# First v weights prepared one unit earlier, and the sample rows' first loads of groups 1 and 2 placed two ticks later

## The chip, the cores and the metric

One core of one Trainium2 chip runs the whole program. The metric is the device time of one execution in microseconds (us); lower is better.

## The reference

One layer of a hybrid decoder is computed for a prompt (1 x 1024 tokens) and for 8 sample sequences of 4 tokens with caches, both with the same weights, width 1024. In short:

```python
h = rmsnorm(x)
q, k, v, z, xbc, dt = split(h @ w_in)
# attention: 12 heads x 64 in 3 dilation groups of 4; per-head RMS norm of q, k; ALiBi;
# (window, dilation) = (128,1), (512,4), (2048,16); the groups are combined by softmax denominators
o_g, lse_g = dilated_attn(q_g, k_g, v_g)       # prompt: blocks of 128; sample: cached keys and values
att = concat(o_g * softmax_g(lse_g))
# SSD: conv(4) + SiLU on xbc, chunked scan (8 chunks, 2 groups), D skip, SiLU(z) gate, norm
y = rmsnorm((ssd(silu(conv(xbc)), dt) + D * xs) * silu(z))
x = x + concat(att, y) @ w_out
x = x + ConvFFN(rmsnorm(x))                    # up, conv(3), SiLU gate, down
```

Outputs are both y, the new key and value rows, the SSM states and the convolution tails.

## The kernel before

Every large product is made of three float32r products: a matrix is split into a high part (`hi`, a cast on ScalarE) and a low part (`lo = raw - hi` on VectorE), and hi·hi, hi·lo and lo·hi are accumulated.

**The projection to q, k, v** is six *slices*: qk and v of group 0, qk and v of group 1, qk and v of group 2. In a slice 9 *units* follow each other (`ORDER`: first the 32 sample rows, then 8 tiles of 128 prompt rows); a unit is 24 matmuls (16 for the sample rows) into one `p_mm` bank (`qkv_unit`). In slice 0 the activations are transposed and split too (`x_load`, `x_tile`). While a slice runs, the weights of the next one are loaded in four quarters (`wq_load`, on SyncE's queue SP) and split in pieces (`wq_split`): 4 pieces for v weights (cast L439 to `wvh`, subtraction L440 to `wvl`), 8 for qk weights (`wqkh`, `wqkl`). In slice 0 the loads of the first v weights come with n = 3 to 6 and the four pieces with n = 5 to 8. VectorE also runs the norms: L615 (sum of squares of a unit), then GpSimd L402 and L403 (rsqrt), then L620 and L621 on VectorE.

**Side work.** Attention, the sample rows and the scan are generators in `Side`. Each `tick` advances every active generator by one `yield`, in the order in which their names were added; what follows a `yield True` is run by the next `pre`, just ahead of the next tick. A qk slice has two ticks in a unit (one in the unit of the sample rows), a v slice one, and each chunk of the later stages three, one behind each third of 24 matmuls. So the order of all instructions is fixed when the program is written; a queue works in that order and never skips.

**Attention of a group** begins with `group_end(g)`: for groups 0 and 1 behind unit n = 1 of the next group's qk slice, for group 2 behind the last v slice, ahead of the xBC chunks. It loads the first two q, k, v tiles of groups 1 and 2 (`qt`, from the scratch `qscr`). `att_gen` then takes one tile: load `qt`, transposes (L670, L671), scores (L686, L689), bias and maximum (L696, with L699 on VectorE), exponentials (L702, ScalarE), transposes of the probabilities (L711), their copies `PT` (L717, L719), the product with v (L727). In group 2 a tile begins with every tick from the third on: tile 2 loads its `qt` in the fifth tick and is transposed in the sixth.

**The sample rows** of a group are `samp_gen(g)`; one runs at a time (width 1). It loads q (`sq_q`, 512 KB: 128 x 1024 f32), a bias (`bl`) and tiles of cached keys (`kt`, 512 KB each, three buffers). One tile of keys takes a GpSimd multiplication (L844), one `yield`, and a VectorE reduction (L846); group 1 has 9 such tiles and group 2 has 3. Then comes a softmax (L814 to L819, with ScalarE's L818), and the same number of value tiles with L851 and L855. Its result goes to `oscr` (L861). `samp_comb` joins the three groups; when it and the attention are through, `comb_gen` runs, and its end (`done.add("att")`) lets the SSD scan begin (`ssd_go`).

`samp_gen(1)` has its first tick right behind `group_end(1)`, `samp_gen(2)` in the third tick behind `group_end(2)`; in the same tick "samp" is advanced ahead of "att", and "kvout" (copies of the new keys and values, L1153) behind it.

**After the scan's first half.** The xBC projection is 12 chunks, then 8 z chunks follow; ahead of z chunk 2 stands a loop that runs ticks with no chunk's matmuls until the SSD of the first head group and its gate are through (`z_chunk`). The scan starts one sequence chunk every two ticks, and one every tick once the last xBC chunk is through (`ssd_go(1)`).

Below, a1, a2, ... are the ticks behind `group_end(1)` (a14 is the last of the qk slice, a15 to a23 those of the v slice), and x1, x2, ... the ticks of the xBC and z chunks and of that loop, from `group_end(2)` on.

Of the kernel before, what the change touches and what calls it, by code (L numbers as in the profile page):

```python
# [302 lines left out]
def body(tc, A):  # L303
# [101 lines left out]
    def r_store(r, scr):  # L405
        ps = p_st()
        T.transpose(ps[:9, :128], r, ident)
        rT = R("rT")
        AC.copy(rT, ps[:9, :128])
        SP.dma_start(scr[0:S].rearrange("(i p) -> i p", p=128), rT[:8])  # L410
        SP.dma_start(scr[S:NT].rearrange("(o p) -> o p", o=1), rT[8:9, :NS])


    def wq_bufs(kind, g):

        n = 512 if kind == "qk" else QN if g == 0 else 256
        return [[None, lo, n, raw] for raw, lo in (R("wqkl" if kind == "qk" else "wvl") for hf in range(2))]

    def wq_load(w, kind, g, q):

        raw = w[q // 2][3][:, q % 2 * 2:q % 2 * 2 + 2]
        src = A["w_in"][0, q * 256:(q + 1) * 256, :].rearrange("(k p) c -> p k c", p=128)
        if kind == "qk":
            for e in range(2):
                c0 = e * 768 + g * 256
                SP.dma_start(raw[:, :, e * 256:(e + 1) * 256], src[:, :, c0:c0 + 256])
        else:
            c0 = 1536 + g * 256
            SP.dma_start(raw[:, :, :256], src[:, :, c0:c0 + 256])
            if g == 0:  # L430
                SP.dma_start(raw[:, :, 256:QN], src[:, :, WIN - 16:WIN])

    def wq_split(w, hf, kks, kind, engine=None):
        _, lo, n, raw = w[hf]
        if w[hf][0] is None:
            w[hf][0] = R("wqkh" if kind == "qk" else "wvh")
        hi = w[hf][0]
        c = slice(kks[0], kks[-1] + 1)
        AC.copy(hi[:, c, :n], raw[:, c, :n])  # L439
        (engine or V).tensor_tensor(lo[:, c, :n], raw[:, c, :n], f32(hi[:, c, :n]), op=ALU.subtract)  # L440

    def pieces(kind):

        if kind == "qk":
            return [(hf, (k,)) for hf in range(2) for k in range(4)]
        return [(hf, (k, k + 1)) for hf in range(2) for k in (0, 2)]
# [3 lines left out]
    def x_load(i):  # L450
        rows = 128 if i < 8 else NS
        xt = R("xt")
        src = A["x_prompt"][0, i * 128:(i + 1) * 128, :] if i < 8 else A["x_sample"].rearrange("b t d -> (b t) d")
        SP.dma_start(xt[:rows], src)
        xts[i] = xt
# [3 lines left out]
    def x_save():  # L459
        while saves:  # L460
            SP.dma_start(*saves.pop(0))

    def x_tile(i):
        rows = 128 if i < 8 else NS
        x_save()
        xt = xts.pop(i)
        c0 = i * 128
        jk = R("jk")
        AC.activation(jk[:rows], xt[:rows], AF.Square, accum_out=ss[:rows, i:i + 1])
        rsqrt_mean(rtok[:, i:i + 1], ss[:, i:i + 1], D, 1)  # L470
        for kk in range(2):
            ps = p_st()
            for j in range(4):
                T.transpose(ps[:, j * 128:j * 128 + rows], xt[:rows, (kk * 4 + j) * 128:(kk * 4 + j + 1) * 128],
                            ident[:rows, :rows])
            pv = ps.rearrange("p (j c) -> p j c", j=4)[:, :, :rows]
            ks = slice(kk * 4, kk * 4 + 4)
            sx = R("sx")[:, :, :rows]
            V.tensor_tensor(sx, pv, g_in[:, ks, None].to_broadcast([128, 4, rows]), op=ALU.mult)
            xr = R("xr")[:, :, :rows]  # L480
            AC.copy(xr, pv)
            saves.append((xscr[:, ks, c0:c0 + rows], xr))
            h = X[0][:, ks, c0:c0 + rows]
            AC.copy(h, sx)
            (V if kk else G).tensor_tensor(X[1][:, ks, c0:c0 + rows], sx, f32(h), op=ALU.subtract)
        if i == 8:
            for p in range(2):
                V.tensor_copy(xsp[:, :, p, :], X[p][:, :, S:NT])
# [141 lines left out]
    def flush(keep=0):  # L630
        while len(stores) > keep:
            d, s = stores.pop(0)
            SP.dma_start(d, s)
# [127 lines left out]
    def per_b(src):  # L761
        return raw_ap(src, 0, [[1024, NB], [0, 16], [1, 1024]])

    def samp_gen(g):
        U = U_S[g]
        q = R("sq_q")
        SP.dma_start(q, per_b(qs[g][0]))
        bl = R("bl")
# [6 lines left out]
        def load(w, c):  # L775
            kt = R("kt")
            if g == 0 and c == 3:
                SP.dma_start(kt[:, :256], raw_ap(qs[0][1 + w], 0, [[256, NS], [0, 4], [1, 256]]))
            elif g == 0:
                n = U0[c + 1] - U0[c]  # L780
                SP.dma_start(kt[:, :n * 256], raw_ap(A["cache_kv0"], w * 256 + U0[c] * 512,
                                                     [[8 * 512, 128], [512, n], [1, 256]]))
            elif c == U - 1:
                SP.dma_start(kt, per_b(qs[g][1 + w]))
            else:
                SP.dma_start(kt, raw_ap(A[f"cache_kv{g}"], w * 256 + c * DIL[g] * 512,
                                        [[32 * 512, 128], [512, 4], [1, 256]]))
            return kt

        order = [(w, c) for w in range(2) for c in range(4 if g == 0 else U)]  # L790
        queue = list(order)
        tiles = {}

        def ahead(n):
            while queue and len(tiles) < n:
                w, c = queue[0]
                if w and c == (3 if g == 0 else U - 1) and ("row", g, 2) not in done:
                    return
                tiles[queue.pop(0)] = load(w, c)

        ahead(1)
        yield
        if g:
            ahead(2)
            yield
            yield
        for w, c in order:
            while (w, c) not in tiles:
# [4 lines left out]
            if w == 1 and c == 0:  # L813
                V.tensor_tensor(sc[:, :U * 16], sc[:, :U * 16], bl[:, :U * 16], op=ALU.add)  # L814
                sv = sc[:, :U * 16].rearrange("p (u e) -> p e u", e=16)
                V.tensor_reduce(m[:, 0:16], sv, op=ALU.max, axis=AX.X, negate=True)
                V.tensor_tensor(sv, sv, m[:, 0:16, None].to_broadcast([128, 16, U]), op=ALU.add)
                AC.activation(sc[:, :U * 16], sc[:, :U * 16], AF.Exp)  # L818
                V.tensor_reduce(m[:, 16:32], sv, op=ALU.add, axis=AX.X)  # L819
                yield  # L820
            if g == 0:
                n = U0[c + 1] - U0[c]
# [340 lines left out]
    for sl, (kind, g) in enumerate(slices):  # L1163
        nxt = slices[sl + 1] if sl < 5 else None
        todo = pieces(nxt[0]) if nxt else []
        for n, i in enumerate(ORDER):
            q = n - (3 if sl == 0 else 0)
            if nxt and q == 0:
                W[nxt] = wq_bufs(*nxt)
            if nxt and 0 <= q < 4:  # L1170
                wq_load(W[nxt], *nxt, q)
            if sl == 0:
                if n + 4 < 9:
                    x_load(ORDER[n + 4])
                if n + 2 < 9:
                    x_tile(ORDER[n + 2])
                if n == 8:
                    x_save()
                    r_store(rtok, rscr)
            qkv_unit(kind, g, i)  # L1180
            flush(2)
            if nxt and n >= (5 if nxt[0] == "v" else 2):
                for _ in range(1 if nxt[0] == "v" or n < 8 else 2):
                    if todo:
                        wq_split(W[nxt], *todo.pop(0), nxt[0])
            if sl == 5:
                if n == 0:
                    stc = R("stc")
                    side.add("states", [states_in("st_in", stc, "state_conv", 24, 4, 12)], 1)
                if n in (1, 3):  # L1190
                    w_load(n // 2)
                if n in (5, 6):
                    w_split(0, n - 5, False)
                if n in (6, 7):
                    w_split(0, n - 6, True)
            side.tick()
            if n == 1 and g and kind == "qk":
                group_end(g - 1)
            if (kind, g) == ("qk", 1) and n == 3:
                side.add("dt", [dt_gen()])  # L1200
            if sl == 1 and n == 0:
                samp_rows(0, 1)
            if sl and n == 4:
                samp_rows(g, 1 if kind == "qk" else 2)
        assert not todo
        if sl == 0:
            side.add("cols", [cols_load()], 1)
        del W[kind, g]
# [678 lines left out]
def build(tc, nc, A):  # L1887
    body(tc, A)
# [24 lines left out]
```

## Time and profile before

| | us |
|---|---|
| three runs | 1652.19, 1644.55, 1650.20 |
| their median | 1650.2 |
| the profiled execution, its own time | 1650.86 |
| its span, first to last instruction | 1648.8 |
| what lies around the span | 2.06 |
| TensorE busy | 1605.4 (97%) |
| VectorE, ScalarE, GpSimd busy | 1010.4, 612.9, 365.0 |
| mean granted TensorE clock | 0.987 of full |

TensorE is the engine that is nearly always busy, so a change counts where TensorE stands still or has its clock lowered. "L711 <- ACT P L702" is to be read as: the instruction of line 711 waited for what ScalarE's line 702 wrote into P. In rows of single instructions the first number is the start, the second the duration; what stands in brackets is how long the engine had been idle before it and which instruction ended that.

### The profile page before, as it was taken

To read this page: it belongs to the slowest core of one execution; us is meant where nothing else is said; L and a number is where in the kernel's file an instruction comes from. 1 tells how busy PE (TensorE), PEld (TensorE's weight loads), DVE (VectorE), ACT (ScalarE), POOL (GpSimd) and SP (SyncE) were. 2 spreads that over 40 slices of the span, in tenths; PEclk is the share of its full clock that TensorE was granted. 3 is DMA by queue.
4 is the path that set the end of the run, shared out by engine and by line. 5 is a ranking of instruction groups with operands and counts; after the bars stand their busy time and mean duration, and the time that the engine had idled before them with its cause. 6 is when DMAs were issued, how large, how long until landed. Compare 5 with 4: busy or idle time off the path is not lost.

```text
span 1648.8 us, 26426 instructions
## 1 busy us (share of the span) xinstructions
PE 1605.4 (97%) x10543; PEld 1520.0 (92%) x10543; DVE 1010.4 (61%) x1714; ACT 612.9 (37%) x1140; POOL 365.0 (22%) x400
## 2 busy tenths in 40 slices
PE   7999998989999899899999999999999999999998
PEld 5787886988998789799999999999999999999998
DVE  5657748656678877753554565564655647555565
ACT  6535524446377874332332322122222221312221
POOL 4554336411025774310111000000000000000000
PEclk9999998999999999899999999999999999999999
DMA  7562366584322317652113111102121020211102
GB/s 231 155 177 75 116 190 198 185 208 125 94 83 85 103 52 208 183 173 67 43 54 103 40 53 39 53 27 65 31 61 53 26 65 14 78 40 39 53 1 106
DMA packets 173897, 154.66 MB, mean 94 GB/s; under 512 B 19554, under 2 KB 152058, under 8 KB 173775
## 3 DMA queue, kind: packets, MB, share of 16 engines
q1 hardware_dynamic: 173775, 152.98, 31.2%
q8 instruction: 83, 1.36, 0.4%
q14 instruction: 39, 0.32, 0.1%
HBM read 124.75 MB, written 31.80 MB: 95 GB/s over the span
## 4 chain that ended last, share of the span: by engine, by line
PE 83%; DVE 5%; ACT 2%; POOL 2%; DMA 2%; issue 1%; SPq 1%; DVEq 0%; ACTq 0%; POOLq 0%
PE p_up L1075 10%; PE p_up L1073 10%; PE p_up L1074 10%; PE p_mm L1073 7%; PE p_mm L1074 7%; PE p_mm L1075 7%; PE p_dn L1847 5%; PE p_dn L1848 5%; PE p_dn L1849 5%; PE p_mm L584 2%; PE p_mm L585 2%; PE p_mm L586 2%; DMA qt<-qscr 1%; PE p_st L727 1%; PE p_st L711 1%
## 5 line engine op out<-in xcount | busy, mean ns | idle before, releaser
L1073 PE MATMUL p_up<-x2h,wh 128*128 128x352 f32 x1032 | 333.4, 323 | 0.0
L1075 PE MATMUL p_up<-x2h,wl 128*128 128x352 f32 x1032 | 333.2, 323 | 0.0
L1074 PE MATMUL p_up<-x2l,wh 128*128 128x352 f32 x1032 | 332.2, 322 | 0.0
L1757 DVE TENSOR_TENSOR fci<-p_up,rb 128x352 f32<-128x352 f32 x129 | 66.2, 513 | 236.5 <-PE p_up L1075 234.9
L1073 PEld LDWEIGHTS p_up<-x2h,wh 128*128 128x128 f32 x1032 | 193.8, 188 | 0.2
L1074 PEld LDWEIGHTS p_up<-x2l,wh 128*128 128x128 f32 x1032 | 193.9, 188 | 0.0
L1075 PEld LDWEIGHTS p_up<-x2h,wl 128*128 128x128 f32 x1032 | 193.6, 188 | 0.0
L1851 DVE TENSOR_TENSOR yacc<-yacc,p_dn 128x352 f32<-128x352 f32 x264 | 133.5, 519 | 75.4 <-PE p_dn L1849 75.4
L1847 PE MATMUL p_dn<-gp,dh 128*128 128x352 f32 x528 | 172.2, 326 | 0.0
L1848 PE MATMUL p_dn<-gp,dh 128*128 128x352 f32 x528 | 171.0, 324 | 0.0
L1849 PE MATMUL p_dn<-gp,dl 128*128 128x352 f32 x528 | 170.7, 323 | 0.0
L1073 PE MATMUL p_mm<-xh,wh 128*128 128x352 f32 x480 | 162.2, 338 | 0.0
L1075 PE MATMUL p_mm<-xh,wl 128*128 128x352 f32 x480 | 155.7, 324 | 0.2 <-DVE wl L1063 0.2
L1074 PE MATMUL p_mm<-xl,wh 128*128 128x352 f32 x480 | 155.3, 323 | 0.0
L1065 ACT CAST wh<-wl 128x512 fp32r<-128x512 f32 (+1 forms) x160 | 92.3, 607 | 125.1 <-PE p_up L1074 76.0
L1063 DVE TENSOR_TENSOR wl<-wl,wh 128x512 fp32r<-128x512 f32 (+1 forms) x160 | 120.9, 756 | 2.7 <-ACT wh L1065 2.6
L1775 DVE SCALAR_TENSOR_TENSOR facc<-fci,cw,facc 128x1072 f32<-128x1072 f32 x88 | 116.8, 1327 | 2.1 <-ACT facc L1767 2.1
L1794 ACT CAST gp<-facc 128x1024 fp32r<-128x1024 f32 (+1 forms) x44 | 25.7, 632 | 216.4 <-DVE facc L1790 216.4
L1847 PEld LDWEIGHTS p_dn<-gp,dh 128*128 128x128 f32 x528 | 99.6, 189 | 0.7 <-DVE yacc L1851 0.7
L1848 PEld LDWEIGHTS p_dn<-gp,dh 128*128 128x128 f32 x528 | 99.2, 188 | 0.0
L1849 PEld LDWEIGHTS p_dn<-gp,dl 128*128 128x128 f32 x528 | 99.1, 188 | 0.0
L1770 POOL COPY nf<-fci 128x18 f32<-128x18 f32 x44 | 9.7, 220 | 396.9 <-DVE fci L1759 396.9
(392 smaller groups left out, 3509.6 us busy)
## 6 DMA issues: line engine op xcount, KB each, us to landing
wl<-in_w_up_dram SPq DMA_DIRECT2D x44, 512.0 KB
dl<-in_w_down_dram SPq DMA_DIRECT2D x22, 512.0 KB
kt<-in_cache_kv_dram SPq DMA_DIRECT2D x20, 512.0 KB
wl<-in_w_in_dram SPq DMA_DIRECT2D x20, 512.0 KB
Ab<-acscr SPq DMA_DIRECT2D x16, 512.0 KB
wqkl<-in_w_in_dram SPq DMA_DIRECT2D x24, 256.0 KB
qscr<-sb SPq DMA_DIRECT2D x24, 256.0 KB
qt<-qscr SPq DMA_DIRECT2D x16, 384.0 KB
```

The source lines that it names most:

```text
L584: T.matmul(ps[:, :n], lhsT=xh, rhs=hi[:, kk, :n], start=first, stop=False)
L1063: V.tensor_tensor(lo[:, c], raw[:, c], f32(hi[:, c]), op=ALU.subtract)
L1065: AC.copy(hi[:, c], raw[:, c])
L1073: T.matmul(ps[:, :CH], lhsT=hi[:, c], rhs=mh[:, c0:c0 + CH], start=k == 0, stop=False)
L1074: T.matmul(ps[:, :CH], lhsT=hi[:, c], rhs=ml_[:, c0:c0 + CH], start=False, stop=False)
L1075: T.matmul(ps[:, :CH], lhsT=lo[:, c], rhs=mh[:, c0:c0 + CH], start=False, stop=k == len(moving) - 1)
L1757: V.tensor_tensor(ci[:, 2 + c0:2 + c0 + w], ps[:, :w], r2t[:, c0:c0 + w], op=ALU.mult)
L1775: V.scalar_tensor_tensor(acc[:, :L], ci[:, i:i + L], cw_f[:, i, fu:fu + 1], acc[:, :L], op0=ALU.mult, op1=ALU.add)
L1847: T.matmul(ps[:, :CH], lhsT=hi[:, mc], rhs=GP[:, s2, c], start=x == 0, stop=False)
L1848: T.matmul(ps[:, :CH], lhsT=hi[:, mc], rhs=GP[:, s2 + 1, c], start=False, stop=False)
L1849: T.matmul(ps[:, :CH], lhsT=lo[:, mc], rhs=GP[:, s2, c], start=False, stop=x == len(fs) - 1)
L1851: V.tensor_tensor(yacc[:, m, c], yacc[:, m, c], ps[:, :CH], op=ALU.add)
```

## The change

Three edits. In slice 0 the loads of the first v weights come with n = 2 to 5 in place of 3 to 6, and their four pieces are split behind units 4 to 7 in place of 5 to 8. `samp_gen` of groups 1 and 2 yields twice before its first load; then both first `kt` tiles are loaded in one step, where the second came one tick behind the first; and one of the two `yield`s between the loads and the first multiplication is gone. Group 0 is as before.

```diff
     def samp_gen(g):
         U = U_S[g]
+        for _ in range(2 if g else 0):
+            yield
         q = R("sq_q")
         SP.dma_start(q, per_b(qs[g][0]))
...
-        ahead(1)
+        ahead(2 if g else 1)
         yield
         if g:
-            ahead(2)
-            yield
             yield
         for w, c in order:
...
         for n, i in enumerate(ORDER):
-            q = n - (3 if sl == 0 else 0)
+            q = n - (2 if sl == 0 else 0)
...
-            if nxt and n >= (5 if nxt[0] == "v" else 2):
+            if nxt and n >= (4 if sl == 0 else 5 if nxt[0] == "v" else 2):
```

## Rows read from the trace of the kernel before

**Rows 1.** The page's chain that ended last: shares of the span by engine.
```profile
PE 83%; DVE 5%; ACT 2%; POOL 2%; DMA 2%; issue 1%; SPq 1%; DVEq 0%; ACTq 0%; POOLq 0%
```

**Rows 2.** TensorE's waits, whole run: total us, times, longest us.
```profile
PE p_st L711 <- ACT P L702: 5.9, 7, 2.8
PE p_st L670 <- DMA qt<-qscr: 4.5, 1, 4.5
...
PE p_mm L590 <- DVE wvl L440: 2.0, 1, 2.0
...
PE p_mm L589 <- ACT wvh L439: 0.5, 1, 0.5
```

**Rows 3.** Stretches: length, busy us and instructions by engine, granted clock, DMA share, GB/s.
```profile
76.00:80.00 4.00, 4.00 (x22) 4.00 (x21) 2.14 (x5) 1.08 (x3) 1.29 (x2) 0.57 0.58 160
...
245.00:260.00 15.00, 12.23 (x58) 8.92 (x57) 14.88 (x28) 5.68 (x18) 12.42 (x8) 0.77 0.65 207
280.00:290.00 10.00, 7.49 (x52) 5.71 (x52) 6.33 (x20) 6.13 (x17) 3.56 (x3) 0.83 0.43 148
...
355.00:360.00 5.00, 4.89 (x20) 4.92 (x21) 0.00 (x0) 3.71 (x9) 2.34 (x2) 0.56 0.77 190
```

**Rows 4.** Instructions at the first slice boundary, VectorE, then TensorE.
```profile
70.20 0.71 DVE L440 TENSOR_TENSOR wvl<-wvl,wvh 128x544 fp32r<-128x544 f32 x1
...
74.66 0.71 DVE L440 TENSOR_TENSOR wvl<-wvl,wvh 128x544 fp32r<-128x544 f32 x1
...
75.44 0.34 PE L590 MATMUL p_mm<-wvl,xsp 128*64 128x272 f32 x1 [2.03 <-DVE wvl L440]
```

**Rows 5.** Instructions at the second slice boundary: GpSimd, VectorE, TensorE.
```profile
89.13 12.31 POOL L829 TENSOR_TENSOR pr<-kt,sq_q 128x768 f32<-128x768 f32 x6 [11.84 <-DMA kt<-in_cache_kv_dram]
...
91.90 1.45 DVE L440 TENSOR_TENSOR wqkl<-wqkl,wqkh 128x512 fp32r<-128x512 f32 x1
...
106.03 0.69 DVE L440 TENSOR_TENSOR wqkl<-wqkl,wqkh 128x512 fp32r<-128x512 f32 x1 [0.69 <-ACT wqkh L439]
...
106.77 0.45 PE L590 MATMUL p_mm<-wqkl,xsp 128*64 128x512 f32 x1 [0.28 <-DVE wqkl L440]
```

**Rows 6.** First attention tile of group 1, then the same step of group 0.
```profile
238.73 4.76 POOL L844 TENSOR_TENSOR kt<-kt,sq_q 128x1024 f32<-128x1024 f32 x2
...
247.37 2.33 DVE L699 TENSOR_SCALAR stt<-stt 128x4 f32<-128x4 f32 x1
...
250.28 1.63 PE L711 MATMUL p_st<-ident,P 128*128 128x128 f32 x4 [2.77 <-ACT P L702]
...
131.12 0.17 DVE L699 TENSOR_SCALAR stt<-stt 128x4 f32<-128x4 f32 x1
...
131.87 1.49 PE L711 MATMUL p_st<-ident,P 128*128 128x128 f32 x4 [0.64 <-ACT P L702]
```

**Rows 7.** The sample softmax of group 1 on ScalarE, and the TensorE wait behind.
```profile
281.10 0.32 ACT L818 ACTIVATE sc<-sc 128x144 f32<-128x144 f32 x1 [7.00 <-DVE sc L817]
...
281.97 0.33 PE L711 MATMUL p_st<-ident,P 128*128 128x128 f32 x1 [1.84 <-ACT P L702]
```

**Rows 8.** SP's issues, group 2's transposes, and the stretch as in rows 3.
```profile
334.32 0.63 SPq L767 DMA_DIRECT2D sq_q<-qs  x1
...
345.84 3.13 SPq L656 DMA_DIRECT2D qt<-qscr  x4
...
345.42 0.33 PE L670 MATMUL p_st<-ident,qt 128*128 128x128 f32 x1
...
355.11 0.45 PE L670 MATMUL p_st<-ident,qt 128*128 128x128 f32 x1 [4.54 <-DMA qt<-qscr]
...
326.00:355.00 29.00, 24.57 (x163) 23.79 (x161) 13.45 (x33) 5.59 (x15) 3.02 (x6) 0.96 1.04 250
```

**Rows 9.** TensorE's first and last tick in the loop ahead of z chunk 2.
```profile
550.64 0.44 PE L1323 MATMUL p_sa<-M,xdt 128*64 128x128 f32 x4 [1.21 <-DVE XSa L1343]
...
561.26 0.69 PE L1323 MATMUL p_sa<-M,xdt 128*64 128x128 f32 x4 [2.71 <-DVE XSb L1343]
```

## The prediction

> **What bounds the kernel now.** First the chain of work that ended last: TensorE holds 83% of it [rows 1], so only its standstills and its low clock can be won. Then TensorE's list of waits [rows 2]. Three entries belong to places that the change touches: L590 and L589 waited 2.0 and 0.5 us for the first v weights; L711 waited for exponentials, 2.8 us at the longest; L670 waited once, 4.5 us, for a `qt` tile. Third the granted clock of the stretches behind these waits, since a standstill is paid twice [rows 3]: 0.57 over 4 us behind the first v weights, 0.77 over 15 us around the first attention tile of group 1, 0.83 over 10 us around the sample softmax, 0.56 over 5 us behind the late `qt` tile. Those are mixtures of the two levels, 1.2 and 2.4 GHz; each time the engine had stood still just before. Lost by the clock: 4 x 0.43 = 1.7, 15 x 0.23 = 3.5, 10 x 0.17 = 1.7 and 5 x 0.44 = 2.2 us.
>
> All sums are made against the profiled execution's own 1650.86 us; it lies 0.7 above the median of the runs, so the same forecast holds for both.
>
> **Part A, the first v weights.** The fourth piece is subtracted at 74.66, TensorE takes it at 75.44 [rows 4]. One unit earlier it takes the place of the third piece, 70.20 to 70.91, about when the slice's first matmuls begin; k = 6 and 7, which it holds, come last among the unit's 16. Eight load DMAs move ahead on SP too, past one activation load each; VectorE's 0.71 moves into units that also split activations, and ScalarE's cast with it. I cost both at nothing: a moved activation tile is wanted two units later, and without that cover the price would be one piece, 0.71. Removed: 2.0 + 0.5 + 1.7 of clock = 4.2.
>
> How much stays? The next boundary needs the last qk piece, now ready at 106.03 + 0.69 = 106.72, waited for by 0.28 [rows 5]. A TensorE 4.2 us earlier wants it at about 102.3. The pieces sit on VectorE between reductions of the sample rows, behind GpSimd's six multiplications, which begin at 89.13 when their DMA has landed and last 12.31, so 2.05 each and up to 101.44. VectorE's third piece runs at 91.90, one reduction behind the first multiplication's end. This chain does not follow TensorE. A seventh multiplication ends at 103.5, the last piece some 0.4 later, 103.9: 2.8 us better, not 4.2. The new standstill of 1.6, in pieces, may lower the clock: 0 to 1.7, I take 1.3. **Part A: -1.5**, between 0 and -4.2.
>
> **Part B, group 1.** The multiplications of `samp_gen(1)` begin at a5, not a4, so one fewer lies ahead of L699. The first two run from 238.73 for 4.76 [rows 6], 2.38 each. L699, a 128x4 operation, takes 2.33 while GpSimd multiplies; in group 0, with GpSimd free, 0.17. It now ends at 249.70; with one multiplication fewer at 247.3, so L711 starts at 247.9 in place of 250.28 and waits 0.4 in place of 2.77. The four L711 are still paced by ScalarE (1.63). Of the 3.5 us of clock I count half, since in group 0 a like start waited 0.64 with L711 spread over 1.49. So -2.4 - 1.7 = -4.1 here.
>
> Most is given back. The 15 us around have VectorE busy for 14.88 [rows 3]; a faster TensorE meets the norm-and-multiplication round of these two engines within two units. The softmax moves from a13 to a14: there L818, which waited for VectorE and held the exponentials for L711 (1.84 [rows 7]), stands ahead of the copies `PT` that the next product needs. I put that wait at about its old size and 2.1 as taken back. **Group 1: -2.0**, between +1 (the moved softmax meets a fuller ScalarE) and -7 (all of 2.77, 3.5 and half of the softmax's 1.84).
>
> The Trainium skill speaks against this edit (SBUF — State Buffer, "Who interferes with whom"): VectorE and GpSimd share a port pair as an exclusive lock, and the later one blocks until the other's instruction ends. The 2.33 against 0.17 agrees. By that alone moving the multiplications only moves the lock, and group 1 would give 0.
>
> **Part B, group 2.** The shift is larger than two ticks. `samp_gen(1)`'s last addition slips from a23 to x1, since the drain behind the v slices does not tick "samp"; so `samp_gen(2)` begins at x4 and loads at x6, where it now loads at x3 and x4. At x1 the addition stands between evacuations on VectorE, ahead of a weight split: 0.2 of TensorE at most. Tile 2's `qt` is issued at x5, now ahead of the four loads `sq_q`, `bl`, `kt`, `kt`: 512 + 72 + 512 + 512 KB = 1.65 MB. From 326 to 355 the DMA moved 250 GB/s at a share above 1 [rows 8], so they take 6.6 us. They were issued from 334.32 on, the `qt` only at 345.84, and it ended the wait at 355.11. Without them it lands near 348.5; TensorE wants it at 355.11 - 4.54 = 350.57. The wait goes, and 2.2 of clock.
>
> What is late next is tile 3: issued at x6 behind these loads, so behind the same bytes as today, 1.6 us (393 KB) after tile 2's present landing, at about 356.6. TensorE wants it one tick after 350.57; the last tick took 5.15 (345.42 to 350.57), the next has one L711 more, so 356.1: a wait of 0.5. **Group 2: -4.5 - 2.2 + 0.2 + 0.5 = -6.0**, between 0 and -6.7.
>
> The DMA page (DMA: Bandwidth & Descriptors, "Where 436 GB/s comes from") puts the ceiling at about 435 GB/s; by it the four loads are worth 3.8 us, the `qt` would land at 351.3 and the gain would be some 0.7 smaller. The measured 250 decides.
>
> **What the shift costs later.** Group 2's sums end at x15, not x13, so the combination and "att" come two ticks later and the scan begins at x29, not x27. From x39 on it starts every tick in either case, so the first half's last chunk slips by one tick only, and the loop ahead of z chunk 2 runs four ticks, not three. It has no matmuls of chunks to fill with: TensorE waited 1.21 in its first tick and 2.71 in its last [rows 9], matmuls behind the latter at the lower clock (0.69 against 0.44). The scan's own matmuls are the same in all, so one more tick costs its idle time: I take 1.7, between 1.2 and 4.4 (2.71 and 1.7 of clock).
>
> **Sum:** -1.5 - 2.0 - 6.0 + 1.7 = -7.8; 1650.9 - 7.8 = 1643.
>
> **Rivals.**
> 1. All of it stays (chance 0.25). For it: behind these stages TensorE is full. -4.2 - 6.0 - 6.7 + 1.2 = -15.7: 1635. Against it: VectorE's 14.88 of 15.
> 2. Tile 3 takes over tile 2's wait (0.17). The loads stand directly ahead of it; if its slack is less than I work out, group 2 gives 0: -1.8, 1649. For it: the same bytes precede it as now. Against: 5.5 us more time.
> 3. The lock only moves (0.10), group 1 gives 0: -5.8, 1645. It is the rule above as a mechanism: 2.33 comes back at the next step.
> 4. Slower (0.05): the late combination. If the loop ahead of z chunk 2 grows by three ticks or more, not one, each at 4.4, the 13.2 outweigh the 9.5 of gains: 1655. Two ticks are the point from which it decides (8.8 against 9.5). For it: the loop is VectorE's and ScalarE's, TensorE cannot fill it. Against: the counted ticks say one.
> 5. The change does not move what it says (0.03): if group 2's loads stayed ahead of tile 2, 1650.9.
>
> **How the numbers follow.** The forecast has 0.40, 1638 to 1647 alone. 0.5% is 8.25 us (about what a measurement of this kernel can tell from no change), so faster means below 1642: two fifths of the forecast (0.16) and rival 1 (0.25), 0.41. Slower by as much means above 1658.5, the far part of rival 4 and what I overlook: 0.05. The rest, 0.54, is within. The range leaves out the fast end of rival 1 and all above 1650: 1633 to 1650.
>
> **What would show it.** After the change L590's 2.0 and L589's 0.5 are gone and a longer wait for `wqkl` stands at the second boundary; L711's longest wait is under 1; L670 on `qt` is under 1; `sq_q` of group 2 is issued behind tile 2's `qt`; the loop ahead of z chunk 2 has four groups of L1323 with no chunk between. I am wrong if the second boundary shows no new wait (then A is larger), if L670 still waits several us, or if the loop has more than four.

## The result, and the profile after

The changed kernel takes 1641.6 us (median of 7 runs, 1639.1 to 1643.9) against 1650.2 before; the ratio is 0.9947, 95% interval 0.9935 to 0.996, so 8.7 us less (6.6 to 10.7). The forecast was 1643, within 1633 to 1650. The profiled execution has a span of 1638.0, 10.8 under that of before.

TensorE's waits after the change, whole run (total us, times, longest us), the answer to [rows 2]:

```profile
PE p_st L727 <- ACT PT L717: 3.1, 2, 2.7
PE p_sa L1323 <- DVE XSb L1343: 2.9, 3, 1.3
PE p_sa L1323 <- DVE XSa L1343: 2.8, 3, 1.2
PE p_mm L590 <- DVE wqkl L440: 2.4, 3, 1.1
...
PE p_st L711 <- ACT P L702: 1.3, 7, 0.3
```

L590 and L589 no longer wait for `wvl` and `wvh`, L670 has no entry, L711's longest wait fell from 2.8 to 0.3. At the places that the change touches two entries are new or grown: 2.4 for `wqkl` at the second boundary (0.6 before) and 2.7 for `PT` behind the softmax of group 1. L1503's entry grew too, from 0.4 to 1.9, but not by the change: with Part A alone, which edits nothing near it, it is 2.0.

Where each microsecond went is seen by taking the same matmul in both traces (same tiles, same occurrence) and subtracting its start before from its start after:

| start before | after minus before | step | what lies between |
|---|---|---|---|
| 60 | +0.67 | | input loads, untouched by the change |
| 84 | -3.85 | -4.5 | first v weights |
| 114 to 127 | +1.13 | +5.0 | second boundary |
| 161 to 246 | -1.12 | -2.25 | first attention tiles of group 0 |
| 260 | -5.85 | -4.7 | first attention tile of group 1 |
| 279 | -4.43 | +1.4 | next tiles of group 1 |
| 298 to 347 | -3.78 | +0.65 | sample softmax of group 1 |
| 369 | -10.19 | -6.4 | tile 2's `qt` |
| 468 | -10.72 | -0.5 | rest of group 2's attention |
| 608 | -10.73 | 0.0 | scan, with the loop ahead of z chunk 2 |
| 663 | -7.91 | +2.8 | end of z, state update |
| 739 to 861 | -9.2 | -1.3 | output projection |
| 880 | -10.78 | -1.55 | its norm |

The last three rows are not the change's, or not shown to be: the kernel with Part A alone (below), which edits nothing behind 110 us, shows +1.5, -1.1 and -1.55 at the same places. The +1.5 is the longer wait at L1503; the rest of the 2.8 is clock, 0.83 over 640 to 650 after the change, and with Part B alone it stayed at 1.00 there behind the same wait. The last row is clock alone: L1628 stands 0.21 in both traces, and the granted clock behind it was 0.80 and 0.86 before, 1.00 after.

**Second boundary.** VectorE, then GpSimd and TensorE, the answer to [rows 5]:

```profile
91.98 0.95 DVE L833 TENSOR_REDUCE sc<-pr 128x12 f32<-128x768 f32 x1 [6.61 <-POOL pr L829]
92.85 1.45 DVE L440 TENSOR_TENSOR wqkl<-wqkl,wqkh 128x512 fp32r<-128x512 f32 x1
...
104.04 1.58 DVE L440 TENSOR_TENSOR wqkl<-wqkl,wqkh 128x512 fp32r<-128x512 f32 x1 [0.69 <-ACT wqkh L439]
```

```profile
90.08 14.99 POOL L829 TENSOR_TENSOR pr<-kt,sq_q 128x768 f32<-128x768 f32 x7 [12.57 <-DMA kt<-in_cache_kv_dram]
```

```profile
101.18 0.45 PE L590 MATMUL p_mm<-wqkl,xsp 128*64 128x512 f32 x1 [0.33 <-DVE wqkl L440]
...
103.41 0.45 PE L590 MATMUL p_mm<-wqkl,xsp 128*64 128x512 f32 x1 [1.12 <-DVE wqkl L440]
...
105.67 0.69 PE L590 MATMUL p_mm<-wqkl,xsp 128*64 128x512 f32 x1 [0.93 <-DVE wqkl L440]
```

The head start that the earlier v weights give VectorE is lost at 85.4: it stands 6.61 us for a reduction that waits, through GpSimd, for `kt`, with the third `wqkl` piece behind it. From there each piece takes its turn behind a multiplication. What the standstill does to the clock, which before was 1.00 from 100 to 116, and what happens at the next meeting, in stretches (columns as in [rows 3]), after, then before:

```profile
104.00:108.00 4.00, 3.02 (x7) 2.03 (x8) 3.12 (x3) 0.82 (x3) 1.06 (x1) 0.50 0.33 129
108.00:112.00 4.00, 4.00 (x14) 3.14 (x13) 1.53 (x2) 1.11 (x2) 1.98 (x3) 0.68 0.00 0
...
132.00:136.00 4.00, 4.00 (x31) 3.28 (x30) 3.93 (x12) 2.58 (x8) 1.40 (x3) 1.00 0.19 67
136.00:140.00 4.00, 4.00 (x26) 3.03 (x25) 2.65 (x10) 0.68 (x3) 1.60 (x2) 1.00 0.00 0
```

```profile
132.00:136.00 4.00, 3.58 (x22) 2.50 (x23) 3.29 (x8) 3.45 (x12) 1.48 (x3) 0.77 0.19 67
136.00:140.00 4.00, 4.00 (x21) 2.88 (x20) 3.03 (x14) 0.00 (x0) 2.35 (x3) 0.81 0.00 0
```

After the boundary TensorE is 1.13 later than before but VectorE's round 0.87 earlier: L699 of group 0's first tile stands at 130.25, in place of 131.12 [rows 6]. So L711 finds its exponentials ready, the 0.64 of wait is gone, and the clock stays at 1.00 over 132 to 140, where it was 0.77 and 0.81. With Part A alone TensorE comes there at the time of before, L699 1.18 earlier, and 1.4 come back: VectorE's earlier round is enough.

**Groups 1 and 2.** GpSimd, VectorE and TensorE at the first attention tile of group 1, the answer to [rows 6]; then ScalarE and TensorE at the softmax [rows 7]:

```profile
238.22 2.38 POOL L844 TENSOR_TENSOR kt<-kt,sq_q 128x1024 f32<-128x1024 f32 x1 [0.60 <-DMA kt<-in_cache_kv_dram]
```

```profile
243.74 2.40 DVE L699 TENSOR_SCALAR stt<-stt 128x4 f32<-128x4 f32 x1
```

```profile
246.73 1.49 PE L711 MATMUL p_st<-ident,P 128*128 128x128 f32 x4 [0.34 <-ACT P L702]
...
283.03 1.43 PE L727 MATMUL p_st<-PT,qt 128*64 128x128 f32 x16 [2.66 <-ACT PT L717]
```

```profile
282.18 0.32 ACT L818 ACTIVATE sc<-sc 128x144 f32<-128x144 f32 x1 [3.24 <-DVE sc L817]
282.40 0.57 ACT L717 COPY PT<-p_st 128x512 f32<-128x512 f32 x1
```

One multiplication, not two, lies ahead of L699. L699 itself still takes 2.40, as with the 2.33 of before: the long duration stayed, only its place is earlier. At the softmax the copy to `PT` now stands behind L818, which waits for VectorE. SP's queue and tile 2's transposes in group 2, the answer to [rows 8], and the loop ahead of z chunk 2 [rows 9]:

```profile
334.05 1.23 SPq L656 DMA_DIRECT2D qt<-qscr  x2
335.32 0.62 SPq L769 DMA_DIRECT2D sq_q<-qs  x1
```

```profile
346.72 0.33 PE L670 MATMUL p_st<-ident,qt 128*128 128x128 f32 x1
```

```profile
537.01 0.44 PE L1323 MATMUL p_sa<-M,xdt 128*64 128x128 f32 x4 [1.20 <-DVE XSa L1343]
...
542.00 0.44 PE L1323 MATMUL p_sa<-M,xdt 128*64 128x128 f32 x4 [1.20 <-DVE XSa L1343]
...
547.00 1.09 PE L1323 MATMUL p_sa<-M,xdt 128*64 128x128 f32 x16 [0.41 <-DVE XSa L1343]
...
551.06 0.44 PE L1323 MATMUL p_sa<-M,xdt 128*64 128x128 f32 x4 [1.14 <-DVE XSb L1343]
```

Tile 2's `qt` is issued ahead of `sq_q`, and L670 takes it without a wait. The loop has four ticks, where it had three.

### The profile page after: what moved, and what is told of

It is laid out like the page before. It is cut to its first block, busy times and chain, and to the rows that moved or that the text cites. A ratio compares the mean times of both kernels' runs of the same rounds, so it can differ in the third digit from the quotient of the medians.

```text
span 1638.0 us, 26430 instructions
## 1 busy us (share of the span) xinstructions
PE 1600.0 (98%) x10543; PEld 1513.6 (92%) x10543; DVE 1007.5 (62%) x1714; ACT 610.5 (37%) x1138; POOL 364.6 (22%) x400
## 4 chain that ended last, share of the span: by engine, by line
PE 82%; DVE 6%; ACT 4%; DMA 2%; POOL 2%; issue 2%; SPq 0%; DVEq 0%; ACTq 0%; POOLq 0%
PE p_up L1075 10%; PE p_up L1073 10%; PE p_up L1074 10%; PE p_mm L1073 7%; PE p_mm L1075 7%; PE p_mm L1074 7%; PE p_dn L1847 5%; PE p_dn L1848 5%; PE p_dn L1849 5%; PE p_mm L584 2%; PE p_mm L586 2%; PE p_mm L585 2%; PE p_st L727 1%; PE p_sa L1323 1%; ACT P L702 1%
```

## The experiments

Each ratio is against the kernel before on the same chip, with its 95% interval; times in us are the ratio's distance from 1 times 1650.

**Part A alone, Part B alone.**

```diff
# a_only: the kernel before with
-            q = n - (3 if sl == 0 else 0)
+            q = n - (2 if sl == 0 else 0)
-            if nxt and n >= (5 if nxt[0] == "v" else 2):
+            if nxt and n >= (4 if sl == 0 else 5 if nxt[0] == "v" else 2):
# b_only: the kernel after with these two lines as before
```

Expected of Part A: 

> Only the first v weights move (loads and splits one unit ahead); the sample rows stay as before. Theory 1 (the second boundary is set by a chain of its own): L590's 2.0 us and L589's 0.5 us for v weights go, with their clock some 4.5 us, but TensorE then waits 2 to 2.5 us in pieces for wqkl at the second boundary and runs at the lower clock behind it; about 2 us stay: 1648, between 1646 and 1650. Rival 1 (all of it stays): 1645.5, waits for wqkl as before (0.6 us in all). Rival 2 (nothing stays): 1650.

Measured: 0.9995 (0.9985 to 1.0005), -0.8 us. L590 waits 2.3 for `wqkl`, the clock is 0.62 over 104 to 108, and the trace shows the three steps of the table again: -4.5 at the first boundary, +3.8 at the second, and then -1.4 more by 161 us. The second step is smaller than in the table because the lower clock behind the boundary cost 1.7 here and 3.4 there. Theory 1 holds for the mechanism. How much stays the times do not settle: 2.2 stay in this trace, but the interval reaches from -2.5 to +0.8, so rival 2 (nothing) is not excluded.

Expected of Part B: 

> Only the sample rows of groups 1 and 2 move; the v weights stay as before. Theory 1: L711's 2.8 us at the first attention tile of group 1 falls under 0.5, L670's 4.5 us for the qt of tile 2 goes; 2 to 3 us come from group 1, 6 to 6.5 from group 2, the late scan costs under 1: 1643, between 1641 and 1645. Rival (the two halves of the change lean on one another, the earlier boundary lets the sample rows run ahead): under 5 us, above 1645.

Measured: 0.9963 (0.9951 to 0.9975), -6.1 us: 1644. Theory 1 holds; its trace has -3.0 for group 1, -6.3 for tile 2's `qt` and 0.0 for the late scan, the same matmuls compared as in the table. The two parts add up to -6.9, and together they measured -8.7; the intervals overlap, so that they help one another is not shown.

**One group alone.**

```diff
# g1_only (g2_only: g == 2): the kernel before with
         U = U_S[g]
+        for _ in range(2 if g == 1 else 0):
+            yield
...
-        ahead(1)
+        ahead(2 if g == 1 else 1)
         yield
         if g:
-            ahead(2)
-            yield
+            if not (g == 1):
+                ahead(2)
+                yield
             yield
```

Expected of group 1 alone: 

> Only group 1's sample rows begin two ticks later; group 2's wait no ticks of their own and still issue their loads ahead of tile 2's qt, since group 1's last addition slips into the xBC chunks and takes them one tick along. Theory 1 (the order of the queue decides): L711's 2.8 us under 0.5, and L670's wait for qt stays at 3 us or more; only group 1's 2 to 3 us are won, less what the loads that now stand closer to qt cost: 1648, between 1646 and 1651. Rival (any later start of these loads would do): L670 waits under 1 us and the time falls to 1642.

Expected of group 2 alone: 

> Only group 2's sample rows begin two ticks later; group 1's stay as before. Their last addition is not moved into the chunks, so group 2's four loads come out at the same tick as tile 2's qt and ahead of it. Theory 1 (the order of the queue decides): L670 still waits 3 us or more, L711 its 2.8 as before: 1650, between 1648 and 1653. Rival (the two ticks alone do it): L670 waits under 1 us, 6 us less: 1644.

Measured: 1.0039 (1.0025 to 1.0053), +6.4, and 1.0068 (1.0043 to 1.0093), +11.2. Both lie above what either theory gave. The `qt` wait stayed, as theory 1 has it, with `sq_q` ahead of tile 2's `qt` in both. Group 1 alone, then group 2 alone:

```profile
352.45 0.30 PE L670 MATMUL p_st<-ident,qt 128*128 128x128 f32 x1 [4.75 <-DMA qt<-qscr]
```

```profile
354.80 0.45 PE L670 MATMUL p_st<-ident,qt 128*128 128x128 f32 x1 [5.05 <-DMA kt<-qs]
```

In the first, L711 waits 0.32 at the first tile of group 1, and that group gives -2.65, as in the table. But each lost 9 to 10 us elsewhere, between 475 and 570: in these kernels group 2's sums end one tick later than before, not two, and the scan begins one tick later.

**The scan one tick late, and two.**

```diff
# comb_1, comb_2: the kernel before with one, two of the added lines
         while ("samp", 2) not in done:
             yield
+        yield
```

Expected: 

> The kernel before, with one idle tick at the start of the sample combination, so that the scan begins one tick later and nothing else moves. Theory 1 (the scan's steps come every second tick, and an odd slip puts them on the wrong ticks beside the chunks): 8 to 10 us more, nearly all of it between 505 and 570 us, as in the two kernels with one group shifted: 1659. Rival 1 (a tick of lateness costs one more tick of the loop ahead of z chunk 2): 1 to 4 us more, 1652. Rival 2 (those two kernels lose by their loads, not by the scan): no change, 1650.5.

> The kernel before, with two idle ticks at the start of the sample combination: the scan begins two ticks later, as after the change, and nothing else moves. Theory 1 (what a slip of the scan costs hangs on which step meets the last convolved chunk, and a slip of two steps past it): the loop ahead of z chunk 2 has four ticks, but no wait of 3 us at 505 to 535; within 1.5 us of the kernel before, 1650.5. Rival (each tick of slip costs alike, about 9 us as the first one did): 15 us or more above, 1666.

Measured: one tick 1.0053 (1.0036 to 1.007), +8.7; two ticks 1.0011 (1.0 to 1.0021), +1.8. The price is not one per tick. ScalarE in the kernel with one tick, then TensorE at the scan's step:

```profile
517.82 1.28 ACT L1261 ACT_TABLE_LOAD   x1
519.12 1.06 ACT L1261 ACTIVATE XSb<-acc 128x1024 f32<-128x1024 f32 x1
...
520.20 2.44 ACT L1308 ACTIVATE M<-Ab,acum 128x128 f32<-128x128 f32 x8
522.66 1.28 ACT L1309 ACT_TABLE_LOAD   x1
523.95 1.06 ACT L1309 ACTIVATE M<-M 128x1024 f32<-128x1024 f32 x1
524.92 1.04 ACT L1310 ACTIVATE Ab<-Ab 128x1024 f32<-128x1024 f32 x1
```

```profile
526.41 0.44 PE L1324 MATMUL p_sa<-M,xdt 128*64 128x128 f32 x4 [1.54 <-DVE M L1315]
...
528.52 0.44 PE L1329 MATMUL p_sa<-Ab,hn 128*64 128x128 f32 x4 [1.67 <-POOL Ab L1316]
```

The finished chunk's Silu (L1261), with a table load of 1.28, stands ahead of the step's `M` and `Ab` (L1309 and L1310, with another 1.28), and the masks are late by 1.54 and 1.67. Three more waits for `M` or `Ab` by 555 us (0.74, 1.19, 1.09) and lowered clock belong to the 8.9 that this trace loses between 468 and 608. In the kernels whose scan begins at the place of before or two ticks later, no step of the scan waits over 0.41 between 475 us and the loop. The same two waits are in both kernels with one group alone. That the order on ScalarE causes them is read from this trace; it was not changed by itself, and it is not enough: before the change the same order stands once, and the step behind it, at 532.56, does not wait.

```profile
518.07 1.28 ACT L1260 ACT_TABLE_LOAD   x1
...
523.06 1.28 ACT L1308 ACT_TABLE_LOAD   x1
```

There the step comes 12 us behind the start of its masks, with one idle tick TensorE wants it 4.7 behind. With two ticks the trace loses 0.0 between 468 and 608; it is 1.3 later already ahead of that, behind a first boundary where the clock cost more (last section).

**The loads' place alone.**

```diff
# ord: the kernel after with
-        for _ in range(2 if g else 0):
+        for _ in range((0, 2, 1)[g]):
...
         while ("samp", 2) not in done:
             yield
+        yield
```

Expected: 

> The kernel after the change, but group 2's loads come one tick earlier, so that they stand directly ahead of tile 2's qt on SP's queue; one idle tick in the combination keeps the scan where it is after the change. Theory 1 (the order on the queue makes the wait): L670 waits 4 to 5 us for tile 2's qt again, its clock falls behind that, 5 to 6.5 us more than after the change: 1647.5. Rival (the wait went because the loads are issued later at all, or because the kernel is earlier there): under 1.5 us of wait, 1642.

Measured: 0.9994 (0.9983 to 1.0004), which is 7.8 us above the 0.9947 of the change (about 5 to 10 by the two intervals; theory 1 gave 5 to 6.5). In the trace 6.8 of it lie at tile 2's `qt`. TensorE in this kernel:

```profile
351.97 0.45 PE L670 MATMUL p_st<-ident,qt 128*128 128x128 f32 x1 [4.54 <-DMA qt<-qscr]
```

The loads were issued at 334.66, within a microsecond of where they are after the change, but ahead of tile 2's `qt` and not behind it. So it is the order on the queue, not the later time. The clock over 350 to 355 fell to 0.54.

**Relieving the second boundary.**

```diff
# s0_1: the kernel after with group 0's first multiplication a tick later
-        for _ in range(2 if g else 0):
+        for _ in range((0, 1, 2)[g]):
...
-        if g:
+        if True:
             yield
# s0_2: two ticks later: (0, 0, 2)[g], and "for _ in range(1 if g else 2):"
```

Expected: 

> The kernel after the change, but group 0's first multiplication and its reductions come one tick later (its loads stay; group 1 waits one tick less, so that from there on all stands as after the change). Theory 1: at the second boundary VectorE is held by a reduction that waits for kt (6.6 us idle in front of it), with the third wqkl piece behind it. With one piece more ahead of that reduction the last piece is ready 2.1 us earlier: TensorE's 2.8 us of waits there fall below 1, the clock stays up from 100 to 111 us, 2 to 5 us less than after the change: 1637 to 1639.5. Rival 1 (the norm round of VectorE and GpSimd sets the place of the first attention tile): the boundary is won but L711 or the norm round takes it back, 1641. Rival 2 (the pieces are paced by GpSimd's multiplications alone): the waits for wqkl stay at 2 us or more, 1641.5.

> As the kernel with group 0's rows one tick later, but two ticks (group 1 then waits none of its own). Theory 1: two pieces stand ahead of the held reduction, the second boundary has no wait left; the same 2 to 5 us as with one tick, up to 1 more: 1636.5 to 1639.5. Rival 1: given back at the first attention tile, 1641. Rival 2: the waits for wqkl stay, 1641.5.

Measured: 0.9964 (0.9951 to 0.9977) and 0.9944 (0.9929 to 0.9959): the first is 2.8 us above the change, with intervals that overlap, the second the same. In the first the boundary was won as theory 1 has it, 4.6 us, with one wait left, and lost again at the next meeting:

```profile
102.90 0.45 PE L590 MATMUL p_mm<-wqkl,xsp 128*64 128x512 f32 x1 [1.14 <-DVE wqkl L440]
129.32 1.48 PE L711 MATMUL p_st<-ident,P 128*128 128x128 f32 x4 [1.96 <-ACT P L702]
```

```profile
130.00:135.00 5.00, 4.64 (x24) 3.66 (x24) 4.77 (x16) 3.00 (x10) 2.36 (x4) 0.66 0.43 132
```

L711 waits 1.96 and the clock falls to 0.66 behind it; 4.9 go there. Another 2.7 go around 148.74, where L727 waits 2.36 for `PT`. In the second 5.1 are won, with one wait of 1.06 left at the boundary, and L711 takes them back:

```profile
130.08 1.10 PE L711 MATMUL p_st<-ident,P 128*128 128x128 f32 x3 [2.49 <-ACT P L702]
```

Rival 1 holds, and for the first kernel it was too mild.

**The softmax of group 1.**

```diff
# exp_late: the kernel after with
-        for _ in range(2 if g else 0):
+        for _ in range((0, 2, 1)[g]):
...
+                if g == 1: yield
                 AC.activation(sc[:, :U * 16], sc[:, :U * 16], AF.Exp)
# exp_late_c: and in group 2 the second kt one tick later
-        ahead(2 if g else 1)
+        ahead(2 if g == 1 else 1)
         yield
+        if g == 2: ahead(2)
```

Expected: 

> The kernel after the change, but in group 1 the exponentials of the sample softmax (L818) are issued one tick behind the subtraction that they wait for (group 2 waits one tick less, so that its loads stay at the same place). Theory 1: the 2.7 us that L727 waits for PT after the change come from L818, which stands ahead of the copy on ScalarE and waits for VectorE; one tick later it finds its input ready: the 2.7 us go, and with them the lower clock behind (0.69 over 5 us, 1.5): 3 to 4 us less, 1638. Rival 1 (VectorE is full there and the next step is late instead): the wait comes back at another instruction, 1641. Rival 2 (the place of the softmax doesn't matter): 2 us or more of wait for PT remain, 1641.5.

> The kernel with the exponentials of group 1 one tick later, and in group 2 the second kt load one tick later still, behind tile 3's qt in place of ahead of it (512 KB less ahead of that tile). Theory 1 (the 2.3 us won at PT were given back as 1.4 us of wait for tile 3's qt and its clock): that wait goes, 1.5 to 2.5 us less than after the change: 1639.5. Rival 1 (some other step gives it back again): 1641.5. Rival 2 (the later kt holds the sample rows up and with them the scan): 1643 or more.

Measured: 0.9946 (0.9931 to 0.996) and 0.9941 (0.9928 to 0.9953); neither can be told from the change. The copy on ScalarE now runs at 279.37, not 282.40, so L818 did hold it; but the other half of `PT` is VectorE's, and it is late as well:

```profile
279.37 0.58 ACT L717 COPY PT<-p_st 128x512 f32<-128x512 f32 x1
...
283.25 0.88 PE L727 MATMUL p_st<-PT,qt 128*64 128x128 f32 x12 [2.00 <-DVE PT L719]
...
352.54 0.30 PE L670 MATMUL p_st<-ident,qt 128*128 128x128 f32 x1 [1.35 <-DMA qt<-qscr]
```

Of the 2.3 us won against the trace of the change, this wait for the next `qt` and the steps around it took 1.65; 0.65 was left at 475 us. With the second `kt` behind tile 3's `qt` that wait is gone, and the trace keeps 2.1 at 475 us; the timed gain, 1 us, is inside the intervals.

**Both at once** (the two-tick edit and the last one together). Expected: 

> Two edits together on the kernel after the change: group 0's first multiplication two ticks later, and group 1's exponentials one tick later with group 2's second kt load behind tile 3's qt. Theory 1 (at each of these meetings TensorE stands where the VectorE and GpSimd round of the sample rows lets it, so an earlier arrival is given back there): within 2 us of the kernel after the change, 1640 to 1642.5. Rival (each edit keeps 1 us or more, hidden by the other's loss until now): 1638 or less.

Measured: 0.9945 (0.9933 to 0.9957), 1640.7 us, as theory 1 has it; the rival's 1638 lies just outside the interval. L711 waits 2.52 at the first tile of group 0 and L727 1.99 for VectorE's half of `PT`. No version beat the change by a margin that can be measured.

## Why the prediction was right, point by point

**Part A, forecast -1.5.** Measured -0.8 alone (-2.5 to +0.8), and -4.5 + 5.0 - 2.25 = -1.8 in the trace. The sum is right through two errors that cancel, and that is luck. The step that failed is the term for the second boundary: 2.7 given back was forecast, 5.0 were (3.8 with Part A alone). The last piece was put at 103.9 and ended at 105.62 (104.04 + 1.58). GpSimd's seven multiplications began 0.95 later than six had before and took 2.14 each, not 2.05, so they ended at 105.07 and not 103.5; the last piece ended 0.55 behind them, where I had 0.4. The clock, 0.50 over 104 to 108 and 0.68 over 108 to 112, cost 3.3 (1.7 with Part A alone) where I took 1.3. What I did not see at all is the other error: VectorE's round comes earlier, so TensorE finds group 0's exponentials ready, and 2.25 come back (1.4 with Part A alone). The first boundary went as worked out, but 1.7 of its 4.5 is clock, which Part B alone did not pay behind the same wait (last section).

**Group 1, forecast -2.0.** Measured -4.7 + 1.4 + 0.65 = -2.65. The first tile went as worked out: L699 earlier by one multiplication, L711's wait 0.34 where 0.4 was forecast. The places of the giving back were right too. At the next tile TensorE comes 5.85 earlier but L699 only 3.55 (253.44 after, 256.99 before), and 1.4 go there; behind the softmax the copies to `PT` stand behind L818 (a wait of 2.66 in place of 1.84). Rival 3 did not come: L699 stayed long, 2.40, and group 1 still gave 2.65.

**Group 2, forecast -6.0.** Measured -6.4 there, and 7.8 when the order alone is put back. Tile 3 did not take the wait over: it waited 0.13 where 0.5 was forecast. That its slack is short shows where the softmax's exponentials came later: TensorE, 2.3 us earlier, waited 1.35 for the next `qt`.

**The late scan, forecast +1.7.** This term was too large. From 468 to 608 us the trace of the change loses 0.0, under the forecast's own lower bound of 1.2, and so do those of Part B alone and of the two ticks alone. The loop has four ticks as counted, but its waits sum to 4.1 where they were 4.5: the added tick's 1.20 is paid by the last tick's wait, 2.71 before and 1.14 after. The lower clock behind the latter is gone as well (0.50 over 561 to 564 before). Timed, two ticks alone cost 1.8, but with an interval from 0 to 3.5.

**Rival 4 was mis-made.** I put the price of a late combination on the loop, 4.4 for each tick that it grows. As far as the traces show, it lies at the step that meets the last convolved chunk, and one tick costs 8.7 where two cost 1.8 (0 to 3.5). Had the two groups' shifts come to one tick, that price would have been about the whole gain; the two together were not measured. My count of ticks said two, and that was right; the 0.05 was too small for what hung on it.

**Sum.** -7.8 forecast, -8.7 timed (-10.7 to -6.6). By the trace the four terms are -1.8 - 2.65 - 6.4 + 0.0 = -10.85, each of them lower than forecast, with 0.5 more in the rest of group 2's attention; +0.67 from the input loads and some clock behind 650 us, which the change doesn't touch, make it -10.8 in all. The timed sum came nearer to the forecast than the terms did. Since the same standstill cost 1.7 us more or less of clock in one profiled execution than in another, that nearness is in part luck.

## What to carry to other kernels

A standstill taken away pays only as far as the next point where TensorE meets another engine's own chain: look there for the price before counting the gain. Here there were three such points in a row. Where several generators share a clock of ticks, a shift has no price per tick; work out which steps of the other generators each count of ticks puts side by side. And on a queue that is full, as this one was, what stands ahead of the wanted transfer counts: 1.65 MB moved from ahead of a tile's load to behind it were worth more than everything else here.

## What the runs showed of the hardware

A table load on ScalarE took 1.28 us. The rows around the second load in the kernel with one idle tick stand 0.02 and 0.01 us apart from it (520.20 + 2.44 to 522.66, 522.66 + 1.28 to 523.95), so here a switch of functions cost the load and no more. The Trainium skill (ScalarE: Activation LUTs, "What ACT_TABLE_LOAD costs") gives 1.283 us for the load, which agrees, and a drain of 1.38 besides, of which these rows show nothing; for this case the rows decide.

The clock does not answer every standstill alike. In the six kernels without Part A, L590 waited 2.03 to 2.05 us at the first boundary, and the lower clock behind it cost 1.7 us in four of them, nothing with Part B alone and 3.4 with the scan two ticks late. Before, Part B alone, two ticks late (columns as in [rows 3]; the clock is 0.79, 1.00 and 0.61):

```profile
76.00:84.00 8.00, 8.00 (x54) 8.00 (x53) 2.14 (x5) 2.12 (x7) 1.29 (x2) 0.79 0.66 178
```

```profile
76.00:84.00 8.00, 7.76 (x62) 7.76 (x63) 2.33 (x6) 2.83 (x8) 2.01 (x3) 1.00 0.67 193
```

```profile
76.00:84.00 8.00, 7.75 (x41) 7.74 (x42) 2.29 (x6) 1.73 (x5) 2.04 (x3) 0.61 0.65 188
```

The same holds for a short one: behind the 0.21 us of L1628 the clock was 0.80 in one profiled execution and 1.00 in another, 1.55 us of difference with no edit near. A step of 1.7 us between two traces can thus be clock alone.
